# Scaling attention probabilities on VectorE or ScalarE, chosen per tile by a list scheduler

## The chip, the cores and the metric

The kernel runs on one core of one Trainium2 chip. The metric is the device time of one execution in microseconds (us), the median of several runs. A core has five engines that run their own instruction streams and meet at semaphores: TensorE (PE in the profile, its weight loads PEld), VectorE (DVE), ScalarE (ACT), GpSimd (POOL) and SyncE (SP), which here issues all DMAs.

## The reference

One layer of an encoder over 2048 tokens of width 1024. A combined projection feeds two mixers, chunked band attention and an mLSTM; their gated outputs are added to the residual stream and a feed-forward block with squared ReLU follows. The change lies in the attention:

```python
scores = jnp.einsum('bclhd,bckhd->bchlk', qc, kband) * (1.0 / math.sqrt(d))
...
scores = scores + bias[None, None]
scores = jnp.where(valid[None, :, None, None, :], scores, -1e30)
p = jax.nn.softmax(scores, axis=-1)
out = jnp.einsum('bchlk,bckhd->bclhd', p, vband)
```

There are 8 heads of width 64; a chunk of 64 tokens sees itself and the 8 chunks before it.

## The kernel before, in words

The 2048 tokens are four blocks of 512 (`NB`), and everything is float32. A matrix product is made of three matmuls on split operands (`mm3`, L644 to L646: high by high, high by low, low by high); a split takes one ScalarE copy for the high half and one VectorE subtraction for the low half (L583 and L585 for weights, L1226 and L1231 for activations). Further large products go through sums of weight or activation blocks (L727, L755).

**Attention.** `unit` handles one head and two of its four 128-token query tiles. For each query tile `scores` makes the scores in one or two PSUM banks (L1417), adds the bias and takes the row maximum on VectorE (L1423, L1429), takes the exponential with its row sum on ScalarE (L1432, where the sum comes out by a second instruction, the accumulator read), inverts the sum on VectorE (L1434) and multiplies the tile by it (L1436). The tiles are 128 rows by 640 columns in blocks 1 to 3, and 128 to 512 columns in block 0. There are 128 of them, held in four pairs of buffers, `sc` (the tile) and `scs` (its small numbers). Then `turn` transposes the probabilities on TensorE (L1448) and splits them while they leave the bank (L1451 on ScalarE, L1453 on VectorE), and `weigh` multiplies them by the values (L1390), adds two halves (L1397 on ScalarE, L1399 on VectorE) and stores the result through the buffers `tmp` to a DRAM tensor `mixa` (L2122).

**What sets the order.** The kernel's code is written as many generators. A generator yields an engine and a price in ns before it issues an instruction, and `Flow` is the list that they stand in. `Flow.run` keeps a clock for each engine, and takes the step that could start first. Where a step names two engines, as in `"act|dve"`, both are candidates at the same price, the one that could start earlier wins, and its name is what the `yield` returns:

```python
for e in th.req[0].split("|"):
    ...
    start = t + self.LAT[frm].get(e, 0.0)
    ...
    key = (max(self.clock[e], start), prio, th.n)
...
self._step(th, e)
```

The prices of `scores` come from `dve2_ns`:

```python
def dve2_ns(n):
    return 70 + 0.55 * n
```

The choices of `Flow` settle which buffers and banks each step gets. Then a second planner, `Order` (L225), takes all instructions with their dependences, prices each anew (`cost`, L267), and fixes for each of the five engines the order in which its instructions stand. Its price for ScalarE is 93 + 0.84 ns for each column, and 190 more with a row sum; for a VectorE instruction with one large operand outside PSUM it is 60 + 0.66 ns for each column. Every engine then works through its own list strictly in that order: an instruction that waits holds up all that stand behind it on its engine, and on SP a DMA that waits for its data holds up the DMAs behind it.

Of the kernel before, what the change touches and what calls it, by code (L numbers as in the profile page):

```python
# [28 lines left out]
ALU = mybir.AluOpType  # L29
# [66 lines left out]
class Flow:  # L96
# [7 lines left out]
               act=dict(pe=220.0, act=130.0, dve=130.0, pool=180.0),  # L104
               dve=dict(pe=220.0, act=130.0, dve=130.0, pool=155.0), pool=dict(pe=290.0, act=130.0, dve=60.0),
# [107 lines left out]
def act_ns(n, ps=False, ap=0):  # L213
    return (51 if ps else 93) + 0.834 * n + 93 * ap


def dve_ns(n):
    return 70 + 1.042 * n


def dve2_ns(n):
    return 70 + 0.55 * n
# [150 lines left out]
class Layer:  # L373
# [1031 lines left out]
    def scores(self, b, i, k, q, bias, sct, ev):  # L1405
        fl, nc = self.fl, self.nc
        e, st = sct
        f = 4 if b == 0 else i
        n = (i + 5 - f) * P
        kf = k.rearrange("p a c -> p (a c)")  # L1410
        halves = 2 if n > 256 else 1
        w = n // halves
        bks = yield "get", self.banks, halves
        yield "pe", 500
        for x in range(halves):
            for y in range(2):
                nc.tensor.matmul(bks[x][:, :w], q[:, y, i * P:(i + 1) * P],  # L1417
                                 kf[:, f * P + x * w:f * P + x * w + w], start=y == 0, stop=y == 1)
        br = bias[:, ::-1]
        j0 = 640 - n  # L1420
        for x in range(halves):
            yield "dve", dve_ns(w)
            nc.vector.tensor_tensor_reduce(  # L1423
                out=e[:, x * w:x * w + w], in0=bks[x][:, :w], in1=br[:, j0 + x * w:j0 + x * w + w],
                op0=ALU.add, op1=ALU.min, scale=-1.0, scalar=3e38, accum_out=st[:, x:x + 1])
            fl.put(self.banks, bks[x])
        if halves == 2:
            yield "dve", 75
            nc.vector.tensor_tensor(st[:, 0:1], st[:, 0:1], st[:, 1:2], op=ALU.min)  # L1429
        mx = st[:, 0:1]  # L1430
        yield "act", act_ns(n, ap=2)
        nc.scalar.activation(e[:, :n], e[:, :n], AF.Exp, scale=-1.0, bias=mx, accum_out=st[:, 2:3])  # L1432
        yield "dve", 75
        nc.vector.reciprocal(st[:, 3:4], st[:, 2:3])  # L1434
        yield "dve", 60 + dve2_ns(n)
        nc.vector.tensor_scalar(e[:, :n], e[:, :n], st[:, 3:4], None, op0=ALU.mult)  # L1436
        fl.set(ev)

    def turn(self, piece, slot, prob, first, ev):
# [1149 lines left out]
```

## Time and profile before

| | before |
|---|---|
| time, median of 3 runs | 2778.67 us (2775.3 to 2782.26) |
| profiled execution, first to last instruction (span) | 2771.8 us |
| TensorE busy | 2749.0 us, 99% |
| VectorE busy | 2056.7 us, 74% |
| ScalarE busy | 1491.5 us, 54% |
| GpSimd busy | 54.7 us, 2% |
| DMA queue, share of 16 engines | 73.0% |
| mean granted TensorE clock | 0.998 |

The span is the profiled execution's own time from its first to its last instruction; the runs' median is 6.9 us above it, for what lies outside the span and for the scatter between executions. Busy time of TensorE counts matmuls that overlap in the pipeline once. The attention runs in two stretches of the span, from some 90 to 485 us and from some 1580 to 1945 us, in which TensorE also works on the projections.

### The profile page before, as it was taken

The numbers are of one execution on the slowest core, as the hardware profiler recorded it, in microseconds if no ns is written. First come the engines' busy times: TensorE is split into PE (matmuls) and PEld (weight loads), VectorE is DVE, ScalarE is ACT, GpSimd is POOL, SyncE is SP. The second block draws the span as 40 slices with busy tenths as digits, with TensorE's granted clock in tenths as the row PEclk, the third lists the DMA queues.
The fourth block names the chain that finished last, engine by engine and source line by source line (L and its number), as shares of the span: only waits on it lengthen the run. The fifth ranks groups of instructions, "written<-read, shape, count | busy, mean of one in ns | idle before, by whom it ended". The sixth has DMA issues, their size and how long they took to land.

```text
span 2771.8 us, 38590 instructions
## 1 busy us (share of the span) xinstructions
PE 2749.0 (99%) x12994; PEld 2285.1 (82%) x12994; DVE 2056.7 (74%) x3783; ACT 1491.5 (54%) x2608; POOL 54.7 (2%) x100
## 2 busy tenths in 40 slices
PE   9999999999999999999999999999999999999998
PEld 7888888888778888888888888888888888888887
DVE  7796789768996866886676688889888656555565
ACT  5564576535454535575555566666335655554443
POOL 0010001000000000000000000000000000000000
PEclk9999999999999999999999999999999999999999
DMA  7968759768765677589877977877977667766574
GB/s 275 294 193 276 230 166 306 248 224 318 258 205 203 220 252 255 194 273 326 289 280 273 296 236 233 257 228 234 290 247 254 209 220 262 242 239 218 190 229 151
DMA packets 329046, 678.64 MB, mean 245 GB/s; under 512 B 36840, under 2 KB 67728, under 8 KB 328848
## 3 DMA queue, kind: packets, MB, share of 16 engines
q1 hardware_dynamic: 328848, 676.18, 73.0%
q8 instruction: 102, 1.67, 0.3%
q14 instruction: 96, 0.79, 0.1%
HBM read 472.59 MB, written 203.44 MB: 244 GB/s over the span
## 4 chain that ended last, share of the span: by engine, by line
PE 94%; DMA 2%; DVE 2%; issue 2%; ACT 0%; SPq 0%; POOLq 0%; POOL 0%; DVEq 0%; ACTq 0%
PE bank L727 44%; PE bank L644 12%; PE bank L645 12%; PE bank L646 12%; PE bank L1417 2%; PE bank L1390 2%; PE bank L1448 2%; PE bank L755 2%; PE bank L1702 1%; PE bank L1703 1%; PE bank L1704 1%; PE bank L1688 0%; DVE wsp L585 0%; DMA r<-u 0%; DMA r<-kfar 0%
## 5 line engine op out<-in xcount | busy, mean ns | idle before, releaser
L727 PE MATMUL bank<-r,wsp 128*128 128x512 f32 x5544 | 1265.6, 390 | 0.9 <-DVE ctx L2083 0.4
L727 PEld LDWEIGHTS bank<-r,wsp 128*128 128x128 f32 x5544 | 1037.9, 188 | 222.3 <-DVE ctx L1869 3.7
L585 DVE TENSOR_TENSOR wsp<-wraw,wsp 128x1024 fp32r<-128x1024 f32 x459 | 561.2, 1223 | 357.6 <-ACT wsp L583 353.3
L583 ACT CAST wsp<-wraw 128x1024 fp32r<-128x1024 f32 x459 | 482.3, 1051 | 506.0 <-PE bank L727 210.6
L644 PE MATMUL bank<-r,wsp 128*128 128x512 f32 x1472 | 586.4, 399 | 1.8 <-ACT r L1226 1.6
L645 PE MATMUL bank<-r,wsp 128*128 128x512 f32 x1472 | 575.2, 391 | 0.2 <-DVE r L1231 0.2
L646 PE MATMUL bank<-r,wsp 128*128 128x512 f32 x1472 | 575.2, 391 | 0.0
L646 PEld LDWEIGHTS bank<-r,wsp 128*128 128x128 f32 x1472 | 276.4, 188 | 58.6
L644 PEld LDWEIGHTS bank<-r,wsp 128*128 128x128 f32 x1472 | 277.0, 188 | 54.1 <-ACT r L1226 1.8
L645 PEld LDWEIGHTS bank<-r,wsp 128*128 128x128 f32 x1472 | 277.2, 188 | 50.7 <-DVE r L1231 0.5
L1869 DVE TENSOR_TENSOR ctx<-bank,ctx 128x512 f32<-128x512 f32 x186 | 127.0, 687 | 89.4 <-PE bank L727 89.3
L1231 DVE TENSOR_TENSOR r<-r 128x512 fp32r<-128x512 f32 x248 | 164.5, 686 | 23.5 <-ACT r L1226 23.0
L1226 ACT CAST r<-r 128x512 fp32r<-128x512 f32 x248 | 149.1, 620 | 51.9 <-DMA r<-u 48.4
L1861 ACT COPY ctx<-bank 128x512 f32<-128x512 f32 x186 | 107.8, 581 | 65.7 <-PE bank L727 62.7
L1432 ACT ACTIVATE sc<-sc,scs 128x640 f32<-128x640 f32 (+4 forms) x128 | 97.4, 762 | 59.8 <-DVE scs L1429 53.8
L2200 ACT ACTIVATE ctx<-ctx 128x512 f32<-128x512 f32 x96 | 60.6, 631 | 103.9 <-DVE ctx L1869 103.9
L1453 DVE TENSOR_TENSOR r<-bank,r 128x512 fp32r<-128x512 f32 (+1 forms) x168 | 97.2, 597 | 18.9 <-ACT r L1451 18.2
L1423 DVE CUSTOM_DVE_ANT_0 sc<-bank,bias 128x320 f32<-128x320 f32 (+3 forms) x240 | 103.5, 462 | 6.4 <-PE bank L1417 4.3
L1451 ACT CAST r<-bank 128x512 fp32r<-128x512 f32 (+1 forms) x168 | 81.9, 518 | 35.6 <-PE bank L1448 28.2
L1390 PE MATMUL bank<-r,r 128*128 128x512 f32 x336 | 95.4, 365 | 2.0 <-DVE r L1453 1.8
L602 DVE TENSOR_TENSOR wraw<-wraw,wraw 128x1024 f32<-128x1024 f32 x76 | 92.9, 1223 | 2.1
L552 DVE TENSOR_TENSOR ctx<-ctx,ctx 128x512 f32<-128x512 f32 x112 | 76.5, 688 | 19.6 <-DMA ctx<-in_wf 12.9
(258 smaller groups left out, 2715.7 us busy)
## 6 DMA issues: line engine op xcount, KB each, us to landing
wraw<-in_wf SPq DMA_DIRECT2D x178, 512.0 KB, 4.4
wraw<-wsum SPq DMA_DIRECT2D x136, 512.0 KB, 4.7
r<-u SPq DMA_DIRECT2D x224, 256.0 KB, 4.3
wraw<-in_w SPq DMA_DIRECT2D x88, 512.0 KB, 5.2
u<-ctx SPq DMA_DIRECT2D x128, 256.0 KB, 2.2
ctx<-in_wf SPq DMA_DIRECT2D x112, 256.0 KB, 4.7
wsum<-ctx SPq DMA_DIRECT2D x112, 256.0 KB, 3.3
u<-tmp SPq DMA_DIRECT2D x96, 256.0 KB, 3.9
```

The costliest lines, as they stand in the source:

```text
L583: nc.scalar.copy(w[:, 0], raw)
L585: nc.vector.tensor_sub(w[:, 1], raw, w[:, 0].bitcast(F32))
L644: mm(ps, lh, rh, start=first, stop=False)
L645: mm(ps, lh, rl, start=False, stop=False)
L646: mm(ps, ll, rh, start=False, stop=last)
L727: mm(ps, wv[:, x, k, n], a[:, y], start=new and k == 0 and x == y == 0, stop=k == 3 and x == 1, skip_group_check=True)
L1226: self.nc.scalar.copy(dst[:, 0], src)
L1231: self.nc.vector.tensor_sub(dst[:, 1], src, dst[:, 0].bitcast(F32))
L1390: nc.tensor.matmul(acc[:, :, c0:c0 + w], st, sl[:, :, o:o + w], start=n == 0, stop=n == total - 1)
L1423: nc.vector.tensor_tensor_reduce(out=e[:, x * w:x * w + w], in0=bks[x][:, :w], in1=br[:, j0 + x * w:j0 + x * w + w], op0=ALU.add, op1=ALU. ...
L1861: nc.scalar.copy(t[:, o:o + 512], ps)
L1869: nc.vector.tensor_add(t[:, o:o + 512], ps, t[:, o:o + 512])
```

## The change

The last step of `scores` names both engines instead of VectorE alone. The price is unchanged. Where the list picks ScalarE, the tile is multiplied there by the inverse sum, one column of 128 numbers, as the activation's scale.

```diff
         nc.vector.reciprocal(st[:, 3:4], st[:, 2:3])
-        yield "dve", 60 + dve2_ns(n)
-        nc.vector.tensor_scalar(e[:, :n], e[:, :n], st[:, 3:4], None, op0=ALU.mult)
+        if (yield "act|dve", 60 + dve2_ns(n)) == "act":
+            nc.scalar.mul(e[:, :n], e[:, :n], st[:, 3:4])
+        else:
+            nc.vector.tensor_scalar(e[:, :n], e[:, :n], st[:, 3:4], None, op0=ALU.mult)
         fl.set(ev)
```

All lines behind it move down by two, so L1451 of before is L1453 of the changed kernel; the ScalarE multiplication is its L1436 and the VectorE one its L1438.

Of the 128 tiles the list now gives 69 to ScalarE: 53 of 640 columns, 3 of 512, 3 of 384, 6 of 256 and 4 of 128. The other 59 stay on VectorE. No other instruction is added or removed on any engine, but both planners run over the new program, and the order changes on all five engines. On TensorE it changes between matmuls that stood at about 97 and 545 us of the span before, and between 1581 and 1945 us; the first 411 and the last 3627 TensorE instructions stand as they did.

**First place: ScalarE, where block 0's attention starts.** The names are the probability tiles `sc` with their row numbers `scs`, split weights `wsp`, transposed probabilities `r`, and a store buffer `tmp`. Before:

```order
L1979 ACTIVATE tmp_110<-bank_129 128x512
L1432 ACTIVATE sc_98,scs_99<-sc_98,scs_99 128x128
L1432 ACTIVATE sc_100,scs_101<-sc_100,scs_101 128x256
L1432 ACTIVATE sc_104,scs_105<-sc_104,scs_105 128x512
L1432 ACTIVATE sc_102,scs_103<-sc_102,scs_103 128x384
L583 CAST wsp_62<-wraw_64 128x1024
L1451 CAST r_84<-bank_129 128x384
```

The same place in the changed kernel:

```order
L1981 ACTIVATE tmp_110<-bank_129 128x512
L1432 ACTIVATE sc_98,scs_99<-sc_98,scs_99 128x128
L1432 ACTIVATE sc_100,scs_101<-sc_100,scs_101 128x256
L1436 ACTIVATE sc_98<-sc_98,scs_99 128x128
L1436 ACTIVATE sc_100<-sc_100,scs_101 128x256
L1432 ACTIVATE sc_104,scs_105<-sc_104,scs_105 128x512
L1432 ACTIVATE sc_102,scs_103<-sc_102,scs_103 128x384
L583 CAST wsp_62<-wraw_64 128x1024
```

Two multiplications stand close behind their exponentials, ahead of the next two exponentials. Over the whole program 8 of the 69 stand right behind their own exponential, 24 have one row between, and 37 have two to seven.

**Second place: the DMA queue of SP, a little later in the same block.** `qfar` and `mixa` are DRAM tensors that are written, `in_w` is the weights and `in_xt` the input. Before:

```order
L2122 DMA qfar<-tmp_110 128x512
L2122 DMA qfar<-ctx_127 128x512
L565 DMA wraw_65<-in_w 128x1024
L2122 DMA mixa<-tmp_109 128x256
L1205 DMA ctx_113<-in_xt 128x512
L2122 DMA mixa<-tmp_108 128x256
```

In the changed kernel:

```order
L2124 DMA qfar<-tmp_110 128x512
L2124 DMA qfar<-ctx_127 128x512
L2124 DMA mixa<-tmp_109 128x256
L565 DMA wraw_65<-in_w 128x1024
L2124 DMA mixa<-tmp_108 128x256
```

The store from `tmp_109` now stands ahead of the load of a weight tile, and the load of `ctx` is no longer between the two stores.

**Third place: TensorE, at about 130 us.** `L644` to `L646` are a projection's matmuls, `L1390` the product with the values, both reading `r` buffers. Before:

```order
L646 MATMUL bank_130<-r_76,wsp_62 128x512
L644 MATMUL bank_130<-r_77,wsp_62 128x512
L645 MATMUL bank_130<-r_77,wsp_62 128x512
L646 MATMUL bank_130<-r_77,wsp_62 128x512
L1390 MATMUL bank_129<-r_84,r_73 128x512
L1390 MATMUL bank_129<-r_84,r_73 128x2x128
L644 MATMUL bank_130<-r_78,wsp_62 128x512
```

In the changed kernel:

```order
L646 MATMUL bank_128<-r_77,wsp_62 128x512
L644 MATMUL bank_128<-r_78,wsp_62 128x512
L645 MATMUL bank_128<-r_78,wsp_62 128x512
L646 MATMUL bank_128<-r_78,wsp_62 128x512
L1390 MATMUL bank_129<-r_84,r_73 128x512
L1390 MATMUL bank_129<-r_84,r_73 128x2x128
L644 MATMUL bank_128<-r_79,wsp_62 128x512
```

The product with the values stands behind one more triple of projection matmuls: what moves on TensorE is which ready work stands where, not how much of it there is.

## The prediction

> **What bounds the kernel now.** I read the page's first part, then the busy times by stretch, then TensorE's waits, then the prices of single instructions, and last the order of the two programs. The page's first lines (busy us, share of the span, instructions):
>
> ```profile
> span 2771.8 us, 38590 instructions
> PE 2749.0 (99%) x12994; PEld 2285.1 (82%) x12994; DVE 2056.7 (74%) x3783; ACT 1491.5 (54%) x2608; POOL 54.7 (2%) x100
> ```
>
> TensorE is idle for 2771.8 − 2749.0 = 22.8 us of the span, 0.8%. Busy alone could hide a slow TensorE, so I looked at its clock, and at its pace in the chain that ended last (start us, us, what):
>
> ```profile
> core 0: 2771.8 us, clock 0.998
> 2700.24 0.23 PE bank L644
> 2700.47 0.23 PE bank L645
> ```
>
> Matmuls of 512 columns follow each other at 0.23 us, at nearly the full clock. TensorE is bound by its own matmuls. The change gives it the same matmuls, so it can only touch the idle time, or add to it. Where that lies, by stretches (TensorE busy, weight loads, VectorE, ScalarE, GpSimd, granted clock, DMA share, GB/s; the cuts are where TensorE's order starts and stops to differ):
>
> ```profile
> 0.00:97.00 97.00, 90.63 (x413) 72.87 (x414) 67.28 (x170) 51.28 (x88) 1.80 (x9) 1.00 0.85 283
> 97.00:546.00 449.00, 445.73 (x2346) 376.67 (x2345) 363.62 (x944) 274.41 (x626) 31.98 (x47) 1.00 0.75 242
> 546.00:1581.00 1035.00, 1030.64 (x4586) 845.61 (x4585) 773.19 (x1100) 533.73 (x797) 2.95 (x7) 1.00 0.74 257
> 1581.00:1946.00 365.00, 364.96 (x2005) 312.67 (x2004) 317.69 (x854) 222.67 (x505) 13.91 (x33) 1.00 0.78 239
> 1946.00:2772.00 826.00, 817.00 (x3651) 677.24 (x3649) 534.93 (x719) 409.39 (x594) 4.03 (x4) 1.00 0.68 229
> ```
>
> The two stretches whose order changes hold 449.00 − 445.73 = 3.27 us and 365.00 − 364.96 = 0.04 us of idle TensorE, 3.3 us together. The other 19.5 us are the start, the end and the middle, where TensorE's order is the same. The view of waits names the four in the first changed stretch (who waited, for whom; us, times, longest); in the second there is none:
>
> ```profile
> PE bank L1390 <- DVE r L1453: 1.8, 1, 1.8
> PE bank L1702 <- DMA r<-mvfar: 0.7, 1, 0.7
> PE bank L1547 <- DVE cum L1543: 0.3, 1, 0.3
> PE bank L644 <- ACT ctx L1681: 0.3, 1, 0.3
> ```
>
> No row says that TensorE waited for a scaled tile (L1436).
>
> **Part 1: what moves from VectorE to ScalarE.** By shapes (busy us, mean ns of one, then the idle time before them and who ended it):
>
> ```profile
> L1432 ACT ACTIVATE sc<-sc,scs 128x640 f32<-128x640 f32 x96 | 79.6, 830 | 47.5 <-DVE scs L1429 47.0
> L1436 DVE TENSOR_SCALAR sc<-sc,scs 128x640 f32<-128x640 f32 x96 | 52.5, 552 | 2.6
> L1432 ACT ACTIVATE sc<-sc,scs 128x512 f32<-128x512 f32 x8 | 5.8, 723 | 4.0 <-DVE scs L1429 4.0
> L1826 ACT ACTIVATE ctx<-ctx,gcol 128x512 f32<-128x512 f32 x12 | 8.5, 718 | 3.2 <-DMA ctx<-x 3.1
> ```
>
> The kernel has no ScalarE multiplication of 640 columns by a per-row number. L1826 is one of 512 at 718 ns, and the exponential of 512, which also takes one number per row, is 723; so I take the exponential's 830 ns for 640. VectorE takes 552. If all 69 tiles were that wide (16 are narrower, so these are upper ends), VectorE loses 69 × 0.552 = 38.1 us and ScalarE gains 69 × 0.830 = 57.3 us. In the changed stretches, 814 us long, VectorE goes from 363.62 + 317.69 = 681.3 to 643.2 us, 84% to 79%, and ScalarE from 274.41 + 222.67 = 497.1 to 554.4 us, 61% to 68%. Neither comes near full. On the path to the end this part costs nothing: TensorE's own work covers it.
>
> The Trainium skill speaks against the move: "ScalarE: Activation LUTs", Rules for kernel authors, sends multiplications to VectorE. The rows agree on the price, 830 against 552 ns. If time followed that price one for one, it would come out slower; the rival on ScalarE's queue below says what has to happen for it.
>
> **Part 2: a wait that may go.** The longest of the four is at 120 us. Rows of the timeline (start, duration, engine, line, and the idle time before with its releaser), of SP's issues, ScalarE, VectorE and TensorE in turn:
>
> ```profile
> 113.16 0.33 SPq L565 DMA_DIRECT2D wraw<-in_w  x1
> 113.63 0.37 SPq L2122 DMA_DIRECT2D mixa<-tmp  x1
> 119.68 0.60 ACT L1979 ACTIVATE tmp<-bank 128x512 fp32r<-128x512 f32 x1 [3.55 <-DMA mixa<-tmp]
> 120.43 0.99 ACT L1451 CAST r<-bank 128x512 fp32r<-128x512 f32 x2
> 121.25 1.15 DVE L1453 TENSOR_TENSOR r<-bank,r 128x512 fp32r<-128x512 f32 x2
> 121.99 0.74 PE L1390 MATMUL bank<-r,r 128*128 128x512 f32 x2 [1.84 <-DVE r L1453]
> ```
>
> So VectorE is only the last link. ScalarE stood 3.55 us at L1979, because its buffer was still being stored; L1451 stood behind it, L1453 behind that, and TensorE waited 1.84 us. Freeing VectorE doesn't help here. But SP's order does: the store of `tmp_109` was behind a weight tile of 512 KB and is now ahead of it, which gets it out sooner (113.63 − 113.16 = 0.47 us of issue alone). The wait costs more than itself, as the clock shows:
>
> ```profile
> 119.50:122.00 2.50, 0.66 (x6) 0.42 (x4) 1.69 (x4) 1.73 (x4) 0.00 (x0) 1.00 0.91 244
> 122.00:126.00 4.00, 4.00 (x15) 3.56 (x16) 3.65 (x20) 1.51 (x6) 0.29 (x2) 0.59 1.03 259
> ```
>
> For 4 us after it the granted clock is 0.59, a loss of 4.00 × 0.41 = 1.6 us. With the wait gone the gain is 1.84 + 1.6 = 3.4 us; if the store still lands late it is nothing, and if a later store takes its place the loss is of the same size. I take half, −1.7 us.
>
> By the Trainium skill ("TensorE: Matmul & The Clock Gate", What's actually happening) the clock falls after an idle window of about 3.4 us. Here 1.84 us was enough to lower it, so the measured 1.6 us stays in the sum; by the rule this wait would cost 1.84 us alone.
>
> **Part 3: the new order in the changed stretches.** Some 2000 TensorE rows stand elsewhere than they did, mostly as the third place in the section on the change shows: a triple of projection matmuls now ahead, now behind an attention product. What waits this order has, the trace of before can't show. From below: none, which takes away all 3.3 us with the 1.6 us of lost clock, −4.9 us. From above: the worse of the two stretches of before had 3.27 + 1.6 = 4.9 us in 449 us; at that rate both have 4.9 × 814 / 449 = 8.9 us, which is +4.0 us over now. The unchanged middle, 1035.00 − 1030.64 = 4.4 us in 1035 us, lies between. I take +1 us, nearer to the upper end, because ScalarE has more to do and, as Part 2 shows, it is the queue whose stalls reach TensorE.
>
> **Sum.** 0 − 1.7 + 1 = −0.7 us. Against the profiled execution that is 2771.8 − 0.7 = 2771.1 us, and against the median of the runs, which lies 6.9 us above the span, **2778 us**: no change. The measurement of this kernel can tell some 0.3%, 8.3 us, from no change (its three runs lie 7.0 us apart). Even the best case, −4.9 us, is within that.
>
> **Rivals.** *All waits in the changed stretches go.* 2778.7 − 4.9 = 2773.8 us. For it: VectorE was the fuller of the two, and the last releaser of the largest wait. Against it: that wait was a late store, and a new order brings its own.
>
> *ScalarE's queue becomes late (slower).* ScalarE runs in order. A multiplication stands behind the exponential that it needs, and in between VectorE must invert the sum:
>
> ```profile
> 111.29 0.19 ACT L1432 ACTIVATION_READ_ACCUMULATOR sc<-sc,scs 128x1 f32 x1
> 111.51 0.17 DVE L1434 RECIPROCAL scs<-scs 128x1 f32<-128x1 f32 x1 [0.28 <-ACT sc L1432]
> 111.71 0.29 DVE L1436 TENSOR_SCALAR sc<-sc,scs 128x128 f32<-128x128 f32 x1
> L585 DVE TENSOR_TENSOR wsp<-wraw,wsp 128x1024 fp32r<-128x1024 f32 x459 | 561.2, 1223 | 357.6 <-ACT wsp L583 353.3
> ```
>
> The round trip is 111.71 − 111.48 = 0.23 us where VectorE is free, and up to 1.22 us more where it is inside a weight split (L585). On VectorE this held up little; on ScalarE everything behind the multiplication stands: the next exponentials, the copies of transposed probabilities (L1451) that TensorE's next product needs, and the weight splits (L583). The two planners price it too low as well: `Flow` takes 60 + 70 + 0.55 × 640 = 482 ns, `Order` 93 + 0.84 × 640 = 631 ns, and the row says 830. `Order` also prices VectorE's at 482 against 552, so ScalarE's is short by 199 − 70 = 129 ns more. If TensorE feels just that for each of the 69, it is 8.9 us; if it feels the whole difference, 69 × 0.278 = 19.2 us. In the middle: 2778.7 + 14 = 2793 us. It decides once TensorE's copies have less lead than such a delay. Against it speaks who waits for whom now:
>
> ```profile
> L1448 PE MATMUL bank<-const,sc 128*128 128x128 f32 x560 | 79.4, 272 | 0.0
> L1451 ACT CAST r<-bank 128x512 fp32r<-128x512 f32 (+1 forms) x168 | 81.9, 518 | 35.6 <-PE bank L1448 28.2 <-DVE scs L1429 3.0 <-DVE scs L1423 2.9
> ```
>
> TensorE's transposes never waited for a tile, and ScalarE spent 28.2 us waiting for TensorE's transposes: it runs ahead, not behind.
>
> *The change does nothing*, because the list finds VectorE free first: 2778.7 us. The order excludes it, with 69 tiles moved.
>
> **How the numbers follow.** My forecast 0.80, all waits gone 0.08, ScalarE late 0.10, nothing done 0.02. Most of the forecast and all of the gain lie within 0.3%. Faster by over 0.3% needs a gain larger than the idle time of the changed stretches, that is, an accident of the measurement or of a stretch that isn't changed: 0.03. Slower: ScalarE late nearly whole, and 0.01 of the forecast, 0.10. Same: 0.87. The range takes the forecast's ends, −4.9 and +4.0 us, with the runs' scatter of 3.5 us below, 2778.7 − 4.9 − 3.5 = 2770 us, and reaches above to the near end of the ScalarE rival, 2778.7 + 8.9 = 2788 us; the rest of that rival is left out.
>
> **What would show it.** Part 1: 69 ScalarE multiplications near 830 ns at 640 columns, ScalarE's busy time up by some 50 us and VectorE's down by some 36, with TensorE's busy time within 2 us. Part 2: in the changed kernel's lines, no wait of L1392 near 120 us, no clock below 1 behind it, and ScalarE's L1981 no longer waiting for `mixa`. Part 3: TensorE's idle time in the two stretches between 0 and 8.9 us. The ScalarE rival would show as TensorE waiting for L1436, L1453 or the weight splits, many times, a few tenths of a us each. The prediction is wrong if TensorE's idle time in these stretches passes some 12 us, or if a wait of several us appears for a DMA that the new order of SP made late.

## The result, and the profile after

The changed kernel takes 2789.68 us (median of 5 runs, 2784.75 to 2790.72) against 2776.87 us before (5 runs, 2774.19 to 2782.26): ratio 1.0034, 95% interval [1.0023, 1.0045]. It is slower by 0.34%, just over what can be told from no change, and 1.7 us above the range. Run again on another occasion it gave 2791.33 us, 1.0049 [1.0036, 1.0062].

The changed kernel's page, first lines (busy us, share of the span, instructions):

```profile
span 2787.9 us, 38559 instructions
PE 2753.7 (99%) x12994; PEld 2287.4 (82%) x12994; DVE 2025.8 (73%) x3714; ACT 1540.1 (55%) x2677; POOL 51.0 (2%) x100
```

ScalarE has 48.6 us more and VectorE 30.9 us less. TensorE was idle for 22.8 us of the span and is now for 2787.9 − 2753.7 = 34.2. Its busy time also rose by 4.7 us with the same matmuls, in part because matmuls at a lowered clock take longer (the two windows of low clock below make 4.1 us, where before had 1.6). By stretches, cut at about the same instructions as before (columns as there):

```profile
97.00:556.00 459.00, 448.27 (x2339) 377.20 (x2338) 349.75 (x915) 292.87 (x654) 29.63 (x47) 0.99 0.74 237
556.00:1595.00 1039.00, 1032.69 (x4592) 846.93 (x4591) 773.30 (x1098) 534.82 (x796) 3.16 (x7) 1.00 0.74 256
1595.00:1962.00 367.00, 365.37 (x2010) 313.74 (x2009) 305.48 (x827) 251.92 (x547) 12.34 (x33) 1.00 0.78 241
```

The first attention stretch is 10 us longer and holds 459.00 − 448.27 = 10.7 us of idle TensorE, where it held 3.3. The second is 2 us longer, the unchanged middle 4. TensorE's waits in the first stretch (who waited, for whom; us, times, longest):

```profile
PE bank L1450 <- ACT sc L1436: 3.8, 2, 3.5
PE bank L1679 <- DMA r<-mfar: 2.7, 3, 1.4
PE bank L1704 <- DMA r<-mvfar: 2.4, 1, 2.4
PE bank L1690 <- DMA r<-mfar: 0.7, 1, 0.7
```

One tile scaled on ScalarE costs 3.5 us. The other three rows are loads from the mLSTM's `mfar` and `mvfar`, which the change doesn't touch.

**Where it accrues.** TensorE's matmuls can be counted. I compare the time of the n-th with that of the n-th in the kernel before, at six counts. Before, these stand at 100, 169, 429, 510, 1511 and 1959 us. Inside a reordered stretch the n-th isn't quite the same matmul, which alone makes a value there uncertain by about 1 us, and each row is one execution. The table gives how many us later TensorE got from one count to the next:

| kernel | 100–169 | 169–429 | 429–510 | 510–1511 | 1511–1959 | start to end |
|---|---|---|---|---|---|---|
| changed | 3.7 | 1.9 | 6.4 | 1.3 | 2.1 | 15.7 |
| changed, run again | 4.6 | 1.3 | 7.3 | 2.0 | 7.3 | 23.0 |
| engine_alone | 2.6 | 0.7 | 0.6 | 0.1 | 3.2 | 8.3 |
| order_alone | 6.5 | 1.1 | 6.1 | −0.4 | 1.5 | 15.4 |
| redraw_up | −0.3 | 0.0 | 6.5 | 1.2 | 2.9 | 10.7 |
| redraw_down | 0.9 | −0.2 | 11.1 | 1.3 | 7.3 | 20.1 |
| all_act | −0.8 | 0.7 | 8.1 | 1.0 | 0.6 | 12.6 |
| late_up | −1.3 | 1.6 | 2.2 | 0.9 | 0.6 | 3.8 |
| late_down | 2.6 | 1.2 | 5.8 | 1.2 | 7.3 | 18.5 |

(The kernels below the second row are the experiments.) All rows are some 3 us too high in sum: the profiled execution of before, 2771.8 us and the 1.8 us that lie outside the span in the runs of both kernels, would be a run of 2773.6 us, under before's median of 2776.87; before_store below, which can't be told from before, has 3.3 us from start to end. The last columns scatter: 2.1 and 7.3 us in two executions of the same kernel, and before_store has 4.1 us in 510–1511. In both rows of the changed kernel two places stand out: 100 to 169 us, where the tile at 118 us lies, and 429 to 510 us.

**The first place.** The changed kernel's timeline, SP's issues, then ScalarE, then TensorE (start, duration, engine, line, and the idle time before with its releaser):

```profile
109.19 2.24 SPq L1276 DMA_DIRECT2D r<-kfar  x2
112.33 0.34 SPq L1324 DMA_DIRECT2D bias<-in_rb  x1
113.18 0.33 SPq L2124 DMA_DIRECT2D qfar<-tmp  x1
113.95 0.32 SPq L2124 DMA_DIRECT2D qfar<-ctx  x1
114.64 0.32 SPq L2124 DMA_DIRECT2D mixa<-tmp  x1
...
120.12 0.60 ACT L1981 ACTIVATE tmp<-bank 128x512 fp32r<-128x512 f32 x1 [4.29 <-DMA mixa<-tmp]
120.61 0.71 ACT L1436 ACTIVATE sc<-sc,scs 128x512 f32<-128x512 f32 x1
...
121.38 1.54 PE L1450 MATMUL bank<-const,sc 128*128 128x128 f32 x6 [3.49 <-ACT sc L1436]
```

The store of `tmp_109` does stand ahead of the weight tile now, but it goes out at 114.64 us, later than the 113.63 of before: loads of `kfar` and a bias load stand in front of it and take SP until then (and TensorE was 0.6 us later than before at 100 us already). ScalarE again stands at L1981 for that buffer, 4.29 us instead of 3.55. Behind L1981 there now stands a scaled tile that TensorE's transposes need at once, so TensorE waits 3.49 us instead of 1.84. The clock goes with it (the changed kernel, columns as above):

```profile
117.00:122.00 5.00, 1.51 (x8) 1.15 (x8) 1.14 (x3) 1.47 (x3) 0.29 (x2) 0.82 0.94 333
122.00:127.00 5.00, 5.00 (x18) 4.23 (x17) 2.09 (x9) 1.72 (x5) 0.29 (x2) 0.50 1.05 255
```

For 5 us the granted clock is 0.50, which costs another 2.5 us.

**The second place.** TensorE's timeline in the changed kernel, its longest waits, and the windows around them:

```profile
457.25 0.63 PE L1679 MATMUL bank<-const,r 128*128 128x128 f32 x4 [0.71 <-DMA r<-mfar]
458.62 1.13 PE L1690 MATMUL bank<-r 128*128 128x128 f32 x8 [0.74 <-DMA r<-mfar]
465.04 0.80 PE L1704 MATMUL bank<-r,ctx 128*128 128x129 f32 x2 [2.37 <-DMA r<-mvfar]
```

```profile
455.00:460.00 5.00, 3.55 (x26) 3.06 (x25) 2.03 (x4) 4.83 (x16) 1.23 (x1) 1.00 1.05 339
460.00:465.00 5.00, 2.31 (x14) 1.50 (x13) 4.96 (x11) 3.35 (x8) 0.00 (x0) 0.99 1.08 328
465.00:470.00 5.00, 4.96 (x25) 4.79 (x26) 1.73 (x5) 0.93 (x2) 0.00 (x0) 0.67 1.06 320
```

TensorE is idle for 4.1 us of 455 to 465, and the clock is 0.67 for the 5 us behind. The DMA engines' share is over 1.0, which made them the first suspect. The kernel before has the same share at the same time, though, and TensorE works without a pause:

```profile
455.00:460.00 5.00, 5.00 (x28) 4.18 (x27) 3.45 (x9) 3.99 (x15) 0.00 (x0) 1.00 1.07 314
460.00:465.00 5.00, 5.00 (x24) 4.12 (x23) 4.93 (x16) 3.12 (x9) 0.00 (x0) 1.00 1.04 377
465.00:470.00 5.00, 5.00 (x32) 4.31 (x31) 4.73 (x9) 5.00 (x12) 1.38 (x1) 1.00 1.06 394
```

So a share over 1.0 alone doesn't make TensorE wait. (From 450 to 455 us, at a share of 1.05, it was idle for 1.0 us.)

### The profile page after: what moved, and what is told of

Read it like the earlier page. It is cut to its first block, busy times and chain, and to the rows that moved or that the text cites. A ratio compares the mean times of both kernels' runs of the same rounds, so it can differ in the third digit from the quotient of the medians.

```text
span 2787.9 us, 38559 instructions
## 1 busy us (share of the span) xinstructions
PE 2753.7 (99%) x12994; PEld 2287.4 (82%) x12994; DVE 2025.8 (73%) x3714; ACT 1540.1 (55%) x2677; POOL 51.0 (2%) x100
## 4 chain that ended last, share of the span: by engine, by line
PE 87%; DMA 6%; DVE 3%; issue 2%; ACT 1%; SPq 0%; POOLq 0%; POOL 0%; DVEq 0%; ACTq 0%
PE bank L727 42%; PE bank L644 12%; PE bank L645 11%; PE bank L646 11%; PE bank L1390 2%; PE bank L1417 2%; PE bank L1450 2%; PE bank L755 1%; DMA r<-u 1%; DMA mfar<-ctx 1%; DVE wsp L585 1%; DMA wsum<-ctx 1%; DMA ctx<-in_xt 1%; DMA r<-qfar 1%; DVE ctx L2042 0%
## 5 line engine op out<-in xcount | busy, mean ns | idle before, releaser
L644 PE MATMUL bank<-r,wsp 128*128 128x512 f32 x1472 | 586.5, 399 | 2.4 <-ACT r L1226 2.2
L646 PE MATMUL bank<-r,wsp 128*128 128x512 f32 x1472 | 575.2, 391 | 0.0
L646 PEld LDWEIGHTS bank<-r,wsp 128*128 128x128 f32 x1472 | 276.6, 188 | 59.1
L644 PEld LDWEIGHTS bank<-r,wsp 128*128 128x128 f32 x1472 | 276.8, 188 | 54.2 <-ACT r L1226 2.9
L1231 DVE TENSOR_TENSOR r<-r 128x512 fp32r<-128x512 f32 x248 | 163.1, 685 | 20.1 <-ACT r L1226 19.6
L1453 ACT CAST r<-bank 128x512 fp32r<-128x512 f32 (+1 forms) x168 | 82.6, 515 | 39.1 <-PE bank L1450 36.5
L1390 PE MATMUL bank<-r,r 128*128 128x512 f32 x336 | 96.3, 366 | 0.0
```

The lines of the kernel that those rows point to most:

```text
L644: mm(ps, lh, rh, start=first, stop=False)
L646: mm(ps, ll, rh, start=False, stop=last)
L1231: self.nc.vector.tensor_sub(dst[:, 1], src, dst[:, 0].bitcast(F32))
L1390: nc.tensor.matmul(acc[:, :, c0:c0 + w], st, sl[:, :, o:o + w], start=n == 0, stop=n == total - 1)
```

## The experiments

Two theories stood at the start: that ScalarE's queue is late (the rival of the prediction), and that the redrawn order makes the loss, whichever engine multiplies. All were timed in five rounds with the kernel before on the same chip. The diffs are shortened.

**1. The engine alone: engine_alone.** The 69 tiles of the changed kernel go to ScalarE, and every other instruction keeps its place of before.

```diff
+# both planners see VectorE's instruction and price; then, for the 69:
+order["DVE"].remove(k)
+o = order["Activation"]
+o.insert(first_with_a_later_planned_begin, k)
```

> The 69 multiplications run on ScalarE, but all other instructions stand on every engine exactly in the order of the kernel before; each moved one stands in ScalarE's order where the planner began it. Theory A (ScalarE's queue: scaled tiles stuck behind other work on ScalarE) says: most of the change's loss is here, +7 us or more against before, with TensorE waiting for the ScalarE multiplication 4 us or more. Theory B (the new order of all five engines) says: within 3 us of before, with such waits under 1 us.

2784.67 us, 1.0023 [1.0015, 1.0032]: 7.1 us, some half to two thirds of the changed kernel's loss, and 4.5 us of waits for the multiplication, which is just what theory A asked for. Its largest wait beside the start's is at the same place. Its waits and ScalarE's timeline there:

```profile
PE bank L1467 <- ACT sc L1452: 4.5, 2, 3.3
```

```profile
121.14 0.60 ACT L1998 ACTIVATE tmp<-bank 128x512 fp32r<-128x512 f32 x1 [4.02 <-DMA mixa<-tmp]
121.63 0.71 ACT L1452 ACTIVATE sc<-sc,scs 128x512 f32<-128x512 f32 x1
```

So moving the tiles costs something in before's order, and its largest wait isn't the multiplication's 0.28 us: one tile came to stand behind a ScalarE row that waits for a store. Whether that tile carries the cost is asked in run 10. The table's row shows 429 to 510 us nearly untouched (0.6). By this run and the next, what the changed kernel loses there isn't the engine's doing.

**2. The order alone: order_alone.** The reverse: all 128 tiles on VectorE, every other instruction in the place that the changed kernel's planners gave it.

```diff
+# both planners see ScalarE's instruction and price for the 69; then:
+order["Activation"].remove(k)
+o = order["DVE"]
+o.insert(first_with_a_later_planned_begin, k)
```

> All 128 multiplications run on VectorE, but all other instructions stand on every engine exactly in the order of the changed kernel. Theory A: the loss is gone, within 3 us of before, no wait near 118 us. Theory B: most of the loss stays, +6 to +10 us, with the waits for mfar and mvfar loads between 450 and 480 us (5.8 us in the changed kernel) still there.

2791.39 us, 1.0048 [1.0033, 1.0063]. The whole loss is there without one multiplication on ScalarE, 6.1 us of it from 429 to 510 us. Its timeline at the first place, ScalarE, VectorE and TensorE:

```profile
120.75 0.60 ACT L1994 ACTIVATE tmp<-bank 128x512 fp32r<-128x512 f32 x1 [5.26 <-DMA mixa<-tmp]
121.38 0.69 DVE L1996 SCALAR_TENSOR_TENSOR ctx<-bank,tmp 128x512 fp32r<-128x512 f32 x1 [5.18 <-ACT tmp L1994]
121.99 0.48 DVE L1449 TENSOR_SCALAR sc<-sc,scs 128x512 f32<-128x512 f32 x1
122.52 1.54 PE L1463 MATMUL bank<-const,sc 128*128 128x128 f32 x6 [5.34 <-DVE sc L1449]
```

The same store holds ScalarE, ScalarE holds VectorE's L1996, and the tile stands behind that: on VectorE the wait is even longer, 5.34 us. The wait's name changes with the engine; its cause, the late store, doesn't.

**3 and 4. Other draws: redraw_up and redraw_down.** The kernel before, all on VectorE, with one price in the list changed by 60 ns either way.

```diff
-        yield "dve", 60 + dve2_ns(n)
+        yield "dve", 120 + dve2_ns(n)   (redraw_up)
+        yield "dve", 0 + dve2_ns(n)     (redraw_down)
```

> The kernel before, with the list's price of the multiplication raised by 60 ns; it stays on VectorE, and both planners make a new order. Theory A: as before, within 3 us, since no tile is scaled on ScalarE. Theory B: a new order alone moves TensorE's waits by several us, so a difference of 4 to 15 us in either direction would not surprise.

> The kernel before, with the list's price of the multiplication lowered by 60 ns; it stays on VectorE, and both planners make a new order. Theory A: as before, within 3 us. Theory B: a second draw of the order, again some us away from before, in either direction.

2783.98 us, 1.0021 [1.0013, 1.003], and 2793.48 us, 1.0052 [1.0039, 1.0065]. Neither changes an instruction; both are slower, one by more than the change. Both lose in 429 to 510 us, 6.5 and 11.1 us.

**5 to 8. DMAs issued sooner at the two places: after_store, after_loads, after_both, before_store.** The fully planned order, with single DMAs moved ahead in SP's list: the store of `tmp_109` by six or seven places, or three loads at 445 to 460 us.

```diff
         for o in order.values():
+# ahead of it, in after_both (after_store: the first; after_loads: the others):
+sp = order["SP"]
+for a, b in [(116, 110), (383, 379), (385, 380), (395, 387)]:
+    sp.insert(b, sp.pop(a))
+# in before_store, on the kernel before: [(116, 109)]
```

> The changed kernel with one DMA moved: the store of tmp_109 to mixa, whose data is ready at 105.32 us in its trace and which SP issues at 114.64, stands six DMAs earlier. All else stands as in the changed kernel. If the store is what holds ScalarE's queue (4.29 us at L1981) and with it the scaled tile: no wait of TensorE near 118 us (3.49 us) and no low clock behind it, 4 to 6 us faster than the changed kernel. If ScalarE is late by its own load: the wait stays.

> The changed kernel with three DMAs moved: two loads from mfar and one from mvfar, which TensorE waits for between 457 and 465 us, stand four, five and eight DMAs earlier, ahead of loads from mixa that are read 16 us later. All else stands as in the changed kernel. If the order of SP's queue is the cause: those waits (0.71, 0.74 and 2.37 us) and the low clock behind them go, 4 to 6 us faster than the changed kernel. If the DMA engines are simply full there: the waits stay or move to the next load.

> The changed kernel with all four DMAs of the two runs before moved. If these two places hold the loss: within 3 us of the kernel before. If the loss is spread over many small waits: still 6 us or more slower.

> The kernel before with its store of tmp_109 to mixa seven DMAs earlier, ahead of the load that it stands behind. The prediction priced the wait at 120 us with its clock at 3.4 us: 3 us faster than before, no wait there and the clock at 1.00. If another late input takes its place: the same time.

after_store: 2788.54 us, 1.0036 [1.0023, 1.0048]. The wait at 118 us goes, and TensorE loses 0.4 instead of 3.7 us from 100 to 169. The whole isn't measurably less: the two intervals are as wide as that gain, and in the profiled execution 510 to 1959 us took 3.7 us more than in the changed kernel's. after_loads: 2788.34 us, 1.0033 [1.0021, 1.0044]. The waits for `mvfar` go, yet 429 to 510 us still loses 6.5 us. after_both: 2784.38 us, 1.0025 [1.0015, 1.0034], 5.6 us behind before, nearer to the loss spread over many waits than to two places that hold it. In both kernels with earlier loads a new wait of 3 us stands in 429 to 510 us. Here ScalarE's timeline and TensorE's waits in after_both:

```profile
454.04 0.63 ACT L1153 ACTIVATE tmp<-tmp 128x512 f32<-128x512 f32 x1 [3.24 <-DMA tmp<-in_x]
```

```profile
PE bank L1693 <- ACT ctx L1656: 2.9, 1, 2.9
```

A load of `in_x` that two of the moved loads have overtaken is now what ScalarE stands at (3.24 us, against 1.12 in the changed kernel), and what TensorE needs stands behind. before_store: 2777.7 us, 0.9995 [0.9986, 1.0004], no difference. The wait at 120 us is gone, and another late input takes its place some 9 us earlier. ScalarE and TensorE in before_store, with the window behind (columns as above):

```profile
110.63 0.63 ACT L1080 ACTIVATE ctx<-ctx 128x512 f32<-128x512 f32 x1 [3.60 <-DMA ctx<-in_xt]
112.64 0.72 PE L1393 MATMUL bank<-r,r 128*128 128x512 f32 x2 [2.25 <-DVE r L1456]
112.00:117.00 5.00, 4.36 (x17) 3.91 (x18) 4.22 (x18) 2.35 (x9) 0.00 (x0) 0.66 1.09 295
```

ScalarE waits 3.60 us for a load of `in_xt`, for which it waited 1.39 us in the kernel before; TensorE waits 2.25 us behind it, and the clock is low again. Why that load is later isn't shown: it is issued ahead of the moved store.

**9. The changed kernel again: after_again.** No edit.

> The changed kernel once more, as the measure for the other runs of this job: 1.0034 times before, 1.0023 to 1.0045, as it was, and TensorE's waits at the same places: the scaled tile near 118 us, loads between 455 and 465 us.

2791.33 us, 1.0049 [1.0036, 1.0062]. The loss is no accident of the first runs; the two intervals overlap.

**10. The engine alone with the store sooner: engine_store.** engine_alone with the store of `tmp_109` seven places earlier.

```diff
+sp.insert(109, sp.pop(116))
```

> Engine alone (69 multiplications on ScalarE, all else in the order of before) and the store of tmp_109 seven DMAs earlier. Engine alone was 1.0023 times before, with 3.32 us of wait for a scaled tile behind a ScalarE row that waited 4.02 us for that store. Theory A in the form that one blocked tile carries the loss of the engine: within 3 us of before, and no wait for the ScalarE multiplication near 119 us. In the form that ScalarE's longer instructions make many tiles late: still 4 us or more slower.

2783.26 us, 1.0015 [1.0005, 1.0025] against engine_alone's 1.0023 [1.0015, 1.0032]: lower, but the intervals overlap. The waits for scaled tiles shrink from 4.5 to 1.1 us, and those for transposed probabilities grow from 1.9 to 3.8; the largest of these, 2.71 us at 113 us, stands where before_store has its new wait. So before_store is the fair comparison: with the store sooner in both, ScalarE costs 0.20%, and without it 0.23%. That the one blocked tile carries the cost isn't borne out, and what does stays open. From 429 to 510 us this execution lost 3.9 us, where engine_alone lost 0.6 and no instruction near there was moved: in that stretch one execution can be off by some 3 us.

**11. All 128 on ScalarE: all_act.**

```diff
-        if (yield "act|dve", 60 + dve2_ns(n)) == "act":
+        if (yield "act", 60 + dve2_ns(n)) == "act":
```

> All 128 multiplications on ScalarE, with the price of the change, and both planners make their order for it. Theory A with many late tiles: about twice the loss of engine alone, 12 us, with waits for the multiplication of 8 us or more. Theory B: a further draw, 5 to 15 us slower like the other three, with waits at loads and stores, and little said by how many tiles ScalarE has.

2789.07 us, 1.0039 [1.0025, 1.0053]. 128 tiles, in an order of their own, cost no more than 69, and among TensorE's waits none is for a scaled tile. The late-queue rival, as a price for each multiplication, would have nearly doubled the cost and asked for 8 us or more of such waits: it falls.

**12. Prices as measured: true_price.** The list compares ScalarE at 813 ns with VectorE at 482 (at 640 columns), where both had 482; it now gives 71 tiles to ScalarE.

```diff
-        if (yield "act|dve", 60 + dve2_ns(n)) == "act":
+        if (yield "act|dve", dict(act=act_ns(n, ap=2), dve=60 + dve2_ns(n))) == "act":
```

> As the change, but the list takes a price for each engine: 93 + 0.834 for each column + 186 ns on ScalarE (813 at 640 columns, where the exponential's row says 830) and 482 on VectorE. If the list's too low price for ScalarE is what costs the time: within 3 us of before. If the new order costs it: slower by 5 us or more, with this price too.

2793.65 us, 1.0053 [1.004, 1.0066]: a price nearer to the trace gave no better order.

**13 to 15. Fewer bytes at 430 to 560 us: before_light, after_light, down_light.** The orders of before, of the changed kernel and of redraw_down are kept; 48 loads bring a quarter of their columns.

```diff
-nc.sync.dma_start(dst, src)
+nc.sync.dma_start(dst[:, :P], src[:, :P])   # both planners count the full load
```

> The kernel before, every instruction in its place, but 48 loads (16 of `in_x`, 32 of the stored normalized activations) bring 128 of their 512 columns, and what is computed from the rest is stale data. Most of these loads lie between 430 and 560 us. Theory A (full DMA engines make the loss of the redrawn orders there; the order of before just escapes it): TensorE has next to nothing to win here, 2775 to 2779 us, no difference. Theory B (the order of the engines makes it): the same. This is the yardstick for the next two runs.

> The changed kernel with the same 48 loads cut to 128 columns, every instruction in its place. Theory A: the stretch between the 2200th and the 2600th matmul, which takes 6.4 us longer than before now, comes within 2 us of before, and the whole to 2780 to 2785 us. Theory B (the order of the engines makes the loss, and loads are late because they are issued late): the stretch stays 5 to 7 us longer and the whole at 2787 to 2792 us.

> The kernel before redrawn by a price lowered by 60 ns, all multiplications on VectorE, with the same 48 loads cut to 128 columns; every instruction stands as in the redrawn kernel. That one loses 11 us between the 2200th and the 2600th matmul and takes 2793.5 us. Theory A: most of the 11 us go, 3 us or less stay, and the whole comes to 2782 to 2786 us. Theory B: 9 us or more stay, and the whole stays above 2790 us.

2776.5 us, 0.9996 [0.9987, 1.0005]; 2785.69 us, 1.0034 [1.0022, 1.0046]; 2790.82 us, 1.0043 [1.0029, 1.0056]. Between 430 and 520 us the bytes fell from 28.3 to 22.9 MB in before, from 26.2 to 22.3 in the changed kernel and from 26.2 to 21.7 in the redrawn one. From 429 to 510 us after_light is still 5.2 us behind before_light (6.4 with all bytes), down_light 10.1 (11.1). The totals of the last two lie near the border of the two expectations, but what the bytes do to the stretch was the point: by this yardstick they make about 1 us of the loss there, and against the kernel before with all its bytes, behind which the two are 3.8 and 8.7 us, some 2.5 us. Most of the loss isn't in these bytes. The theory isn't excluded by that: from 440 to 470 us the DMA engines' share still is 0.99 to 1.09 in down_light and 0.87 to 1.02 in after_light, and run 10 shows how far one execution can be off here. In down_light TensorE's waits in 420 to 530 us are these, none of them directly for a load:

```profile
PE bank L657 <- ACT ctx L1683: 3.5, 1, 3.5
PE bank L657 <- ACT r L1239: 1.1, 1, 1.1
PE bank L1715 <- DVE ctx L1703: 1.1, 1, 1.1
```

Behind the second a load stands all the same. ScalarE's L1239 waited for a sum on VectorE, and the sum for a load from `mixa`:

```profile
462.44 0.69 DVE L999 TENSOR_TENSOR tmp<-tmp,r 128x512 f32<-128x512 f32 x1 [2.08 <-DMA tmp<-mixa]
```

Ahead of the first, the 3.5 us, VectorE was busy for all of 450 to 460 us, and ScalarE's queue stood behind it.

**16 to 18. The second planner alone: late_up, late_down, after_late.** The list's choices and all buffers stay. Only `Order`'s price for the multiplications changes, by +60 and −60 ns in the kernel before, and by +190 ns for the 69 on ScalarE in the changed one.

```diff
         self.dur = [self.cost(i, e) for i, e in zip(self.ins, self.eng)]
+        for k, i in enumerate(self.ins):
+            if self.eng[k] == "DVE" and self.scaled(i):
+                self.dur[k] += 60   # late_down: -60; after_late: "Activation", 190
```

> The kernel before, all 128 multiplications on VectorE, the list and its buffers as before; only the second planner counts 60 ns more for each of them (482 to 542 ns at 640 columns, where the trace has 552). Some 80 of TensorE's 12,696 rows move and some 250 of VectorE's. Theory A (any redraw of the order loses, buffers or not): 2782 to 2790 us, with waits of 1 to 5 us that before doesn't have. Theory B (the loss comes with the list's other choice of buffers and banks): within 3 us of before.

> The same with 60 ns less (422 ns at 640 columns). Theory A: 2782 to 2790 us. Theory B: within 3 us of before.

> The changed kernel with the list's choices as they are; only the second planner counts 190 ns more for each of the 69 ScalarE multiplications (631 to 821 ns at 640 columns, where the trace has 830). Theory A: another draw with the same buffers, 2783 to 2793 us. Theory B (the buffers make the loss): it stays at 2787 to 2792 us. Theory C (the second planner's short price made the loss, since everything behind a multiplication on ScalarE was planned too early): 2777 to 2782 us.

2780.68 us, 1.0009 [1.0001, 1.0018]; 2787.95 us, 1.0044 [1.0032, 1.0057]; 2796.52 us, 1.0075 [1.0062, 1.0089]. late_up is within 3 us of before, as the second expectation has it; late_down isn't. It moves some tens of TensorE's 12,994 rows and no buffer, and loses as much as the change. TensorE's waits from 420 to 530 us, first in late_down, then in late_up:

```profile
PE bank L1711 <- DMA r<-mvfar: 4.0, 1, 4.0
```

```profile
PE bank L1674 <- ACT ctx L1660: 1.6, 1, 1.6
PE bank L1711 <- DMA r<-mvfar: 0.8, 1, 0.8
PE bank L1686 <- DMA r<-mfar: 0.3, 1, 0.3
```

The same matmul waits 4.0 us in the one and 0.8 in the other, over a price 60 ns up or down. Other buffers aren't needed for the loss. The third theory falls too: giving the multiplications on ScalarE nearly their true price in the second planner made it slower still.

## Why the prediction was wrong, point by point

**What bounds the kernel**: right. The granted clock is near 1 outside the waits, and of the 16.1 us that the span grew 11.4 are idle TensorE; the other 4.7 are longer busy, in part by the low clock.

**Part 1, what moves**: the durations were right. The changed kernel's groups by shape (busy us, mean ns, then idle time and its releaser):

```profile
L1436 ACT ACTIVATE sc<-sc,scs 128x640 f32<-128x640 f32 x53 | 43.3, 829 | 2.5 <-DVE scs L1434 2.3
L1438 DVE TENSOR_SCALAR sc<-sc,scs 128x640 f32<-128x640 f32 x43 | 23.7, 552 | 1.3
```

829 ns against the 830 taken. ScalarE's sum is as foretold (48.6 for some 50 us), VectorE's a little smaller (30.9 for some 36), and TensorE's is not within 2 us, in part because of the clock. That it costs nothing holds for the changed kernel's order, in which order_alone without those 69 isn't faster. It doesn't hold by itself: in before's order the engine costs 0.23%, some 6 us, a term that the prediction put at nothing. The two losses don't add: 0.23 and 0.48% would be 0.71, and the changed kernel has 0.34 and 0.49 in its two measurements.

**Part 2, the wait at 120 us**: wrong in sign. The step that failed is "SP's order does": a place in a list was read as a time. The store stands ahead of the weight tile, but other loads stand ahead of both, and it went out 1.0 us later, not 0.47 sooner. The wait grew from 1.84 to 3.49 us, and with the low clock from 3.4 to 6.0: +2.6 us where −1.7 was taken, so this term was off by 4.3 us. after_store, which does bring the store out sooner (107.67 us), takes the wait away. In before_store, though, another wait of 2.25 us came in its place, so taking the wait away won nothing there, and "With the wait gone the gain is 1.84 + 1.6 = 3.4 us" isn't borne out either. (The L1392 of the prediction's signs is L1390 in the changed kernel: lines shift only behind the edit.)

The Trainium skill's rule on the clock ("TensorE: Matmul & The Clock Gate", What's actually happening: it falls after an idle window of about 3.4 us, and the window runs freely) can't be read as a safe length of a single wait: 1.84 us gave 0.59, 3.49 us gave 0.50, and several waits together, the longest 2.37 us, gave 0.67. In redraw_up a wait of 2.49 us left the clock at 1.00, and one of 1.23 us was followed by 0.57 (rows in the last section).

**Part 3, the new order**: the mechanism was named, and its size was wrong; this is the step that failed most. It took +1 us, with +4.0 as the upper end, from "at that rate both have 8.9 us". The rate was that of before's own order. The two stretches now hold 10.7 + 1.6 = 12.4 us of idle TensorE, the mark beyond which the prediction called itself wrong; with the low clock of the two windows, which the 8.9 counted too, it is 16.5. Of the 15.7 us that the profiled execution lost, 12.0 lie outside 100 to 169 us, 6.4 of them from 429 to 510 us. What the runs put in place of the rate: seven other draws of the order were made beside the changed kernel's. The four that leave all tiles on VectorE (redraw_up, redraw_down, late_up, late_down) are 0.21, 0.52, 0.09 and 0.44% slower than before, the three others (all_act, true_price, after_late) 0.39, 0.53 and 0.75%. Before's order is the fastest of these nine (TensorE idle for 22.8 us of the span, in the eight others for 28.6 to 38.8), and one draw's waits say little about the next's. Why before's is the best, by luck or by an earlier choice, no run shows. The range would have had to reach to about +0.75%, 2799 us.

**The rivals.** ScalarE late: its sign was right, its mechanism only in part. TensorE did wait for L1436, but three times, 4.8 us in all and 3.5 of them for one tile; not many times by a few tenths. Nor were the planners' short prices the reason: in after_late, with nearly the true price in the second planner, it waited 5.2 us. All waits gone and nothing done: no.

**The sum.** The time between span and median, put at 6.9 us, was mostly scatter: a span of 2787.9 us belongs to a run of 2789.68, so 1.8 us lies outside. The sum also takes the wait at 120 us twice: Part 2 takes half of its 3.4 us off, and both ends of Part 3 are reckoned from the same wait. Without Part 2's −1.7 us it would have been +1 us, still far from the 12.8 measured.

**Open.** Which chain of instructions decides in 429 to 510 us isn't settled. Every redraw loses there, from 2.2 to 11.6 us, but the last link differs: loads of `mfar` and `mvfar`, a ScalarE row behind a load of `in_x`, a sum on VectorE. Bringing three loads forward moved the wait and didn't remove it; fewer bytes took some 1 to 2.5 us, and what part of the rest full DMA engines have isn't known. What ScalarE costs in before's order, some 0.2%, isn't traced to a wait either. No version tried is measurably faster than the kernel before.

## What to carry to other kernels

Where a planner fixes the whole program's order, an edit that frees an engine is also a new draw of that order; draw a few without the edit (a price up and down) before sizing the edit, because that scatter, here 0.1 to 0.5% without the edit, may be larger than anything the edit can win. Separate the two by moving the instructions with the order held, and by taking the new order without the move. And read when a DMA goes out from the trace, with all that stands ahead of it on its queue: being ahead of one large load says nothing alone. A wait that is taken away may be followed by another: measure the whole, as in before_store.

## What the runs showed of the hardware

A queue that works in order makes one late store a wait on any engine: held 4 to 5 us at a row that waits for `mixa`, ScalarE passed that on to whatever stood behind, directly (3.49 us) or by way of VectorE (5.34 us). A DMA share of 1.05 to 1.08, as from 455 to 470 us, looked like the limit, yet the kernel before has 1.04 to 1.07 there with TensorE busy all the time, and taking 15 to 19% of the bytes out of 430 to 520 us took away some 1 to 2.5 of 6 to 11 us.

A short wait of TensorE can cost nearly twice itself: 3.49 us of idle were followed by 5 us at clock 0.50, another 2.5 us, and 1.84 us by another 1.6. Its length doesn't tell whether it will. Two waits in redraw_up, the first with the window behind it at full clock, the second with a low one (columns as above):

```profile
458.49 0.55 PE L1677 MATMUL bank<-const,r 128*128 128x128 f32 x3 [2.49 <-DMA r<-mfar]
459.00:469.00 10.00, 9.69 (x52) 7.99 (x51) 8.80 (x20) 7.17 (x20) 0.00 (x0) 1.00 1.01 316
470.74 1.37 PE L644 MATMUL bank<-r,wsp 128*128 128x512 f32 x3 [1.23 <-ACT r L1226]
471.00:475.00 4.00, 4.00 (x11) 2.77 (x11) 3.93 (x10) 3.49 (x9) 1.38 (x1) 0.57 0.46 165
```
